# Matmul with batch normalization on one core: the task order as a table, and one block turned by the DMA

## The chip, the core and the metric

The kernel runs on one core of a Trainium2 chip. The metric is device time in microseconds (us), the median of three runs. The profile is of one further execution; its span is the time from its first to its last instruction.

## The reference

```
x: (16, 512, 1024) float32     weight: (1024, 768) float32     gamma, beta: (768,)
y = np.matmul(x, weight)
mean = np.mean(y, axis=(0, 1), keepdims=True)
var = np.var(y, axis=(0, 1), keepdims=True)
y_norm = (y - mean) / np.sqrt(var + eps)
return (gamma * y_norm + beta).astype(np.float32)
```

So it is a product of 8192 by 1024 with 1024 by 768, then every one of the 768 columns is normalized with its mean and variance over all 8192 rows. No value of a column can be written before the last row of that column has been multiplied.

## The kernel before

The 8192 rows of x are 16 chunks (c = 0 to 15) of 512 rows, and the 768 columns are six column tiles (nt = 0 to 5) of 128. x is read with a conversion to bf16 through GpSimd's DMA queue into a buffer called `ring`, transposed there by VectorE into `xT_sb`, and multiplied by the weight in bf16.

Tiles 0 and 1 are multiplied with rows of x as the stationary side while x comes in (line 510); their chunks 14 and 15 are done by columns (line 814) and turned at lines 1064 and 1074. Tiles 2 to 5 have the columns on the partitions (`y_ps` is 128 columns by 512 rows, line 575): each product of a chunk takes eight matmuls, in two tasks of four. VectorE takes the statistics of the chunk (`bn_stats`, line 711; ScalarE for most of tile 2), ScalarE writes it to `y_sb` as bf16 (line 715). When all 16 chunks of a tile are done, the mean and variance give a scale and a shift (`finish_tasks`), and the tile is written out in eight blocks of two chunks, 1024 rows by 128 columns, 512 KB each, while TensorE goes on with the next tile. Tile 5 comes last; nothing of it can leave before its last matmul.

A block has its columns on the partitions and must be turned before it is stored. There are three ways:

- `raw_turn` and `raw_block`: the block is turned before its statistics are known, and normalized afterwards by VectorE (multiply, line 1174) and GpSimd (add, line 1178). `raw_spread` first turns the scale and shift (lines 1141, 1142), gathers and deals them (line 1145) and puts them in PSUM (line 1158).
- `col_block` with mode `pe`: VectorE normalizes in place (line 1026), TensorE turns the block with eight transpositions by the identity (line 1044), ScalarE copies the result from PSUM to a part of `ring` as float32 (line 1210), SP stores it (line 1202). A matmul task can host these transpositions: one is put behind each of its matmuls.
- `col_block` with mode `xact`: VectorE (for tile 2 ScalarE, line 1023) normalizes, SP issues one DMA transposition of the whole block from `y_sb` to a part of `ring` in bf16 (line 1220), ScalarE converts that to float32 in another part of `ring` (line 1232), SP stores it (line 1202).

For tile 4, the fifth column tile, blocks c = 0, 2 and 4 are raw, c = 6, 8, 10 and 12 are of mode `pe`, and c = 14 is held back and stored in two halves at the end of the matmuls (`held_block`, copies at line 1252, stores at line 1255). For tile 3, the blocks c = 2 to 14 are of mode `xact`.

At the end the statistics of tile 5 are joined (line 1308), ScalarE takes the root (line 1311), VectorE the reciprocal and the final pair (lines 1323, 1324), and each block of tile 5 is normalized (line 1348), turned by TensorE (line 1044), copied by ScalarE (line 1361) and stored by SP (line 1364). This is 4 MB that leaves after the last matmul.

`ring` has 6144 words of 4 bytes in each partition. A block's float32 result takes 1024 words, the bf16 result of a DMA transposition 512. A piece is free again when its store has landed.

The order of the work is set while the program is built. Every piece of work is a `Task` with the engines that may do it, its dependencies and a due time. `arrange` goes forward in a planned time: it looks at which engine can begin something first, and among the tasks that could begin on it within 0.2 us takes the one that is due first. The instructions are emitted in that order, so each engine's queue, SP's too, is fixed; an instruction whose data is not there holds up all behind it on its engine.

In the following a task is named by its engine's letter (P for TensorE, V for VectorE, A for ScalarE, G for GpSimd, S for SP) and its number in the order in which the tasks are made. Those used are:

- A562, A566, A570, A574: conversions (line 1232) of blocks c = 8, 10, 12, 14 of tile 3; S563, S567, S571, S575: their stores. S565, S569, S573: DMA transpositions of c = 10, 12, 14.
- V644, A645, A647: the scale and shift of tile 4 turned (lines 1141, 1142), gathered (line 1145), put in PSUM (line 1158). V648, G649, S650: multiply, add and store of raw block c = 0 of tile 4; V651 to S653: c = 2; V654 to S656: c = 4.
- V657, 658, A659, S660: block c = 6 of tile 4, normalized, turned, copied, stored. V661 to S664: block c = 8; V665 to S668: c = 10; V669 to S672: c = 12.
- A684: chunk 6 of tile 5 to `y_sb` (line 715). V691: statistics of chunk 8 of tile 5.
- A725: the root of tile 5 (line 1311). A731 and A734, S732 and S735: copies and stores of the held block.
- S739, S743, S747 and so on: the eleven stores of tile 5.

Of the kernel before, what the change touches and what calls it, by code (L numbers as in the profile page):

```python
# [97 lines left out]
class Wires:  # L98
# [8 lines left out]
    def ready(self, queue):  # L107
        lanes = self.lanes[queue]
        return 0.0 if len(lanes) < self.LANES else lanes[-self.LANES]
# [9 lines left out]
        return t, land  # L119


def arrange(tasks, turns, log=None):

    free = {e: 1.25 for e in ("PE", "DVE", "ACT", "POOL", "SP")}
    wires = Wires()
    port = {"DVE": 0.0, "POOL": 0.0}
    left = sorted(tasks, key=lambda t: t.prio)
    order = []  # L130
    SEM, LOOK = 0.06, 0.2

    def ready(t):
        if t.after is not None and t.after.end is None:
            return None
        r = 0.0
        for d in t.deps:
            if d.end is None:
                return None
            r = max(r, d.end + SEM + t.slack)  # L140
        kept = [(s.pool, s.pool.mark()) for s in t.takes] if len(t.takes) > 1 else []
        fits = True
        for s in t.takes:
            p = s.pool.place(s)
            if p is None:
                fits = False
                break
            r = max(r, p[0] + SEM)
            if kept:
                s.pool.take(s, p[1])  # L150
        for pool, mark in reversed(kept):
            pool.reset(mark)
        if not fits:
            return None
        if t.dma:
            r = max(r, wires.ready(list(t.engines)[0]))
        return r

    def start_of(t, r, e):

        b = max(r, free[e])
        if e == "DVE" and t.lock:
            b = max(b, port["POOL"])
        elif e == "POOL" and not t.dma:
            b = max(b, port["DVE"])
        return b

    while left:
        seen = [(t, ready(t)) for t in left]
        first = {}  # L170
        for t, r in seen:
            if r is not None:
                for e in t.engines:
                    b = start_of(t, r, e)
                    if e not in first or b < first[e]:
                        first[e] = b
        if not first:
            raise RuntimeError(f"nothing can begin: {[(t.prio, t.emit) for t in left[:8]]}")
        e = min(first, key=lambda k: first[k])
        best = None  # L180
        for t, r in seen:
            if r is not None and e in t.engines and start_of(t, r, e) <= first[e] + max(LOOK, t.look):
                if best is None or t.prio < best[1]:
                    best = start_of(t, r, e), t.prio, t
        start, _, t = best
        for s in t.takes:
            s.pool.take(s, s.pool.place(s)[1])
        occ, lat = t.engines[e]
        t.hosted = []
        if t.hosts:  # L190
            room = t.hosts
            for u, r in seen:
                if u in turns and r is not None and r <= start + 0.3 and room >= 1:
                    n = min(room, turns[u][0])
                    if turns[u][0] == turns[u][1]:
                        places = [s.pool.place(s) for s in u.takes]
                        if any(p is None or p[0] > start for p in places):
                            continue
                        for s in u.takes:
                            s.pool.take(s, s.pool.place(s)[1])  # L200
                        u.takes_done, u.takes = u.takes, []
                    t.hosted.append((u, n))
                    turns[u][0] -= n
                    room -= n
                    occ += 0.0555 * n
                    lat += 0.0555 * n
        if t in turns:
            occ = lat = 0.0555 * turns[t][0]
            lat += 0.2
            t.count = turns[t][0]  # L210
        free[e] = start + occ
        if e == "DVE" and t.lock or e == "POOL" and not t.dma:
            port[e] = start + occ
        t.end = start + lat
        if t.dma:
            free[e], t.end = wires.send(e, start, occ, t.dma, t.count)
        t.start, t.engine = start, e
        order.append(t)
        left.remove(t)
        for u, n in t.hosted:  # L220
            if turns[u][0] == 0:
                u.end = t.end + 0.2
                left.remove(u)
    return order


# [1 line left out]
def kernel(  # L228
# [19 lines left out]
    P = 128  # L248
# [24 lines left out]
    XT, YB, SQ = C - EARLY, 28, 3  # L273
    ADDED = (0,6,16,28,40)
    PARTED, LATE, SINGLE = (4,5,7,8,9,10), (12,13,14,15), (2,3,6)
    MODE = {2:'xact',3:'xact',4:('pe',)*8}
    MODE = {nt: m if isinstance(m, tuple) else (m,) * (C // GY) for nt, m in MODE.items()}
    RAW, RAWADD, RAWDUE = {2:(0,2),3:(0,),4:(0,2,4)}, {2:'POOL',3:'POOL',4:'POOL'}, {2:14.0,3:8.0,4:8.0}
    RING = 3 * CH // 32 * KQ // 2
# [85 lines left out]
    def act(occ):  # L365
        return {"ACT": (occ, occ + 0.11)}
# [73 lines left out]
    order = [("x", 0), ("w", 0, 2), ("x", 1), ("w", 2, 4)]  # L440
# [5 lines left out]
    t = 1.0  # L446
# [238 lines left out]
    def y_of(nt, c):  # L685
        return y_col.setdefault((nt, c // GY), Slot(ys))
# [174 lines left out]
    S = clock[0]  # L861
# [94 lines left out]
    k = 0  # L956
# [74 lines left out]
    def turn_block(prio, nt, m0, count, deps, uses):  # L1031

        bank = Slot(banks)
        todo = []

        def step():
            if not todo:
                o_ps = psum.tile([P, count, P], bf16, tag="b")
                bank.tile = o_ps
                for s in range(count):  # L1040
                    c, i = divmod(m0 // P + s, RT)
                    todo.append((o_ps[:, s], y(nt, c)[:, i * P:(i + 1) * P]))
            dst, src = todo.pop(0)
            seq(nc.tensor.transpose(dst, src, ident))  # L1044

        def emit(eng):
            for _ in range(emit.task.count):
                step()

        emit.step = step  # L1050
        t = task(prio, pe(0.0555 * count), emit, deps, takes=[bank], uses=uses)
        emit.task = t
        turns[t] = [count, count]
        return t, bank
# [136 lines left out]
    def col_block(nt, c, due, fin_task, held=False):  # L1191
# [26 lines left out]
        def xbar(eng):  # L1218
# [49 lines left out]
    for nt in range(GA, NT - 1):  # L1268
# [10 lines left out]
        f = finish_tasks(nt)  # L1279
        start = clock[0] + 3.0  # L1280
# [58 lines left out]
    for c, r0, rows in ends:  # L1339
        due = E + 2.0 + 0.6 * c  # L1340
        n = max(rows // CH, 1)
# [13 lines left out]
        b, bank = turn_block(due + 0.6 * (n - 1), nt, m0, count, norms, [y_of(nt, c + i) for i in range(n)])  # L1355
# [7 lines left out]
        def store(eng, slot=slot, m0=m0, count=count):  # L1363
# [48 lines left out]
```

## Time and profile before

| | |
|---|---|
| median of 3 runs | 206.11 us (205.88 to 206.58) |
| span of the profiled execution | 204.1 us |
| around the span, against the median | 2.0 us |
| TensorE busy | 189.3 us (93%) |
| VectorE, ScalarE, GpSimd busy | 159.3, 146.2, 124.1 us |
| DMA: read and written in HBM | 36.71 MB, 25.17 MB |
| last matmul of the product ends | 186.6 us |
| SP issues the first store of tile 5 | 189.31 us |

The times in the profile are microseconds from the first instruction of the profiled execution. The time of that execution outside its span is not given; the difference of 2.0 us between its span and the median of the runs stands for it. The column "DMA" counts the mean busy share of the core's 16 DMA engines, "GB/s" what they moved; in the rows for a window of time they are given in 40 equal slices of that window. A DMA's semaphore is raised in 16 parts, one for each DMA engine, and the DMA has landed with the last of them.

### The profile page before, as it was taken

The numbers are of one execution on the slowest core, as the hardware profiler recorded it, in microseconds if no ns is written. First come the engines' busy times: TensorE is split into PE (matmuls) and PEld (weight loads), VectorE is DVE, ScalarE is ACT, GpSimd is POOL, SyncE is SP. The second block draws the span as 40 slices with busy tenths as digits, with TensorE's granted clock in tenths as the row PEclk, the third lists the DMA queues.
The fourth block names the chain that finished last, engine by engine and source line by source line (L and its number), as shares of the span: only waits on it lengthen the run. The fifth ranks groups of instructions, "written<-read, shape, count | busy, mean of one in ns | idle before, by whom it ended". The sixth has DMA issues, their size and how long they took to land.

```text
span 204.1 us, 3510 instructions
## 1 busy us (share of the span) xinstructions
PE 189.3 (93%) x1210; PEld 114.5 (56%) x1210; DVE 159.3 (78%) x250; ACT 146.2 (72%) x260; POOL 124.1 (61%) x150
## 2 busy tenths in 40 slices
PE   7969999999999999999999999999999999997900
PEld 3457554657488888777865444444444445544600
DVE  4031879999999999969989998987999878657900
ACT  2001461368989999899978766999998959956950
POOL 7776954877499989997403999389613312940000
PEclk9999999999999999999999999999999999999965
DMA  4999999999999999999686899899999999999998
GB/s 71 172 199 196 176 196 196 196 197 197 190 193 197 197 196 196 196 197 195 103 181 200 297 339 336 248 301 328 295 322 227 336 303 274 347 343 310 310 347 253
DMA packets 98562, 48.74 MB, mean 239 GB/s; under 512 B 24304, under 2 KB 98032, under 8 KB 98544
## 3 DMA queue, kind: packets, MB, share of 16 engines
q0 software_dynamic: 34624, 18.36, 65.5%
q1 hardware_dynamic: 63920, 30.16, 52.6%
q8 instruction: 9, 0.15, 0.3%
q14 instruction: 9, 0.07, 0.1%
HBM read 36.71 MB, written 25.17 MB: 303 GB/s over the span
## 4 chain that ended last, share of the span: by engine, by line
PE 86%; ACT 3%; DMA 3%; POOL 2%; issue 1%; ACTq 0%; DVE 0%; POOLq 0%
PE y_ps L575 54%; PE y_ps L510 24%; PE y_ps L814 4%; ACT o_sb L1361 3%; DMA ring<-in_x_dram 3%; PE o_ps L1044 1%; POOL ring L403 1%; POOL w_sb L387 1%; PE y_ps L753 1%; PE a_ps L903 1%; PE o_ps L1074 0%; ACTq L1407 0%; PE idle_ps L591 0%; PE tot_ps L871 0%; ACT ring L1252 0%
## 5 line engine op out<-in xcount | busy, mean ns | idle before, releaser
L575 PEld LDWEIGHTS <-w_sb 128*128 128x128 bf16 x520 | 50.3, 97 | 57.6
L575 PE MATMUL y_ps<-xT_sb,w_sb 128*128 128x512 bf16 (+1 forms) x272 | 59.3, 371 | 0.0
L575 PE MATMUL y_ps<-x_pl,w_sb 128*128 128x512 bf16 x248 | 57.4, 379 | 0.0
L403 POOL DMA_DIRECT2D ring<-in_x_dram x76 | 47.2, 626 | 14.4 <-DMA ring<-in_x_dram 5.5
L510 PE MATMUL y_ps<-w_sb,xT_sb 128*128 128x256 bf16 x448 | 50.6, 273 | 1.7 <-DMA ring<-in_x_dram 1.6
L510 PEld LDWEIGHTS <-xT_sb 128*128 128x128 bf16 x448 | 43.5, 98 | 9.4 <-DVE xT_sb L435 2.9
L435 DVE STREAM_TRANSPOSE xT_sb<-ring 128x1024 f32<-128x1024 f32 (+1 forms) x29 | 31.2, 1111 | 14.1 <-DMA ring<-in_x_dram 13.9
L711 DVE BATCH_NORM_STATS2 stats<-y_ps 128x6 f32<-128x512 f32 x46 | 30.9, 687 | 7.7 <-PE y_ps L575 7.2
L715 ACT CAST y_sb<-y_ps 128x512 bf16<-128x512 f32 x51 | 29.0, 593 | 10.4 <-DVE stats L711 6.3
L547 ACT COPY x_pl<-xT_sb 128x1024 bf16<-128x1024 bf16 x32 | 32.8, 1063 | 1.7 <-DVE xT_sb L435 1.7
L942 POOL TENSOR_TENSOR ring<-ring,sum 128x1024 f32<-128x1024 f32 (+1 forms) x11 | 23.8, 2188 | 14.9 <-ACT y_ps L724 10.9
L659 ACT ACTIVATE sq_sb<-y_ps 128x512 f32<-128x512 f32 x28 | 16.3, 610 | 16.2 <-PE y_ps L510 15.9
L666 POOL TENSOR_TENSOR sum<-sum,sq_sb 128x512 f32<-128x512 f32 x20 | 25.6, 1278 | 3.0 <-ACT sq_sb L659 1.7
L662 DVE TENSOR_TENSOR sum<-y_ps,sum 128x512 f32<-128x512 f32 x28 | 18.9, 675 | 6.3 <-ACT sq_sb L659 5.3
L672 ACT CAST y_sb<-y_ps 128x512 bf16<-128x512 f32 x28 | 16.3, 594 | 8.2 <-DVE sum L662 8.0
L1178 POOL TENSOR_TENSOR ring<-ring,sum 128x1024 f32<-128x1024 f32 x6 | 14.8, 2477 | 9.8 <-issue 8.5
L937 DVE TENSOR_TENSOR ring<-y_sb,a_ps 128x1024 f32<-128x1024 bf16 (+1 forms) x16 | 16.7, 1079 | 0.1
L1044 PE MATMUL o_ps<-ident,y_sb 128*128 128x128 bf16 x104 | 13.1, 221 | 1.6 <-DVE y_sb L1348 1.5
L1232 ACT CAST ring<-ring 128x1024 f32<-128x1024 bf16 x13 | 13.8, 1063 | 0.6 <-DMA ring<-y_sb 0.6
L1145 POOL COPY sum<-sum 32x256 f32<-32x256 f32 (+1 forms) x17 | 5.8, 340 | 13.4 <-DVE sum L1142 6.5
L428 DVE STREAM_TRANSPOSE xT_sb<-ring 128x2048 bf16<-128x2048 bf16 x6 | 13.5, 2290 | 0.1
L591 PE MATMUL idle_ps<-idle_sb 128*128 128x512 f32 x18 | 9.6, 688 | 1.5 <-DVE idle_sb L316 1.5
(104 smaller groups left out, 153.7 us busy)
## 6 DMA issues: line engine op xcount, KB each, us to landing
out_dram<-ring SPq DMA_DIRECT2D x37, 512.0 KB, 3.4
ring<-in_x_dram POOLq DMA_DIRECT2D x52, 256.0 KB, 8.8
out_dram<-o_sb SPq DMA_DIRECT2D x6, 512.0 KB, 4.7
ring<-in_x_dram POOLq DMA_DIRECT2D x16, 128.0 KB, 5.9
w_sb<-in_weight_dram POOLq DMA_DIRECT2D x8, 192.0 KB, 6.2
out_dram<-ring SPq DMA_DIRECT2D x6, 256.0 KB, 3.0
ring<-in_x_dram POOLq DMA_DIRECT2D x4, 192.0 KB, 7.8
out_dram<-o_sb SPq DMA_DIRECT2D x3, 256.0 KB, 2.5
```

The lines of the kernel that those rows point to most:

```text
L403: bi = seq(nc.gpsimd.dma_start(x_bf[32 * i:32 * i + 32], src[:, :, KQ * i:KQ * (i + 1)]))
L435: seq(nc.vector.transpose(dst, src[:, :, jw0:jw1]))
L510: seq(nc.tensor.matmul(y_ps[:, s], x_of(c, jw, e, t * P, (t + 1) * P), w_sb[:, jw, e, 0:NA], start=(s == 0 and jw == 0 and e == 0), stop=( ...
L547: seq(nc.scalar.copy(dst, pairs) if eng == "ACT" else ENG[eng].tensor_copy(dst, pairs))
L575: seq(nc.tensor.matmul(y_ps, w_sb[:, jw, e, nt * P:(nt + 1) * P], moving(c, jw, e, q0 * QR, q1 * QR, parted), start=(jw == 0 and e == 0 an ...
L659: seq(nc.scalar.activation(sq_sb[:, 0:n], slot.tile[:, 0:n], AF.Square))
L662: seq(nc.vector.tensor_add(sum1, slot.tile[:, 0:n], sum1))
L666: seq(ENG[eng].tensor_add(acc, acc, state["sq"][:, 0:n]))
L711: seq(nc.vector.bn_stats(dst, slot.tile))
L715: seq(nc.scalar.copy(y(nt, c), slot.tile))
L937: seq(nc.vector.tensor_mul(slot.o, y_row[c].y[:, s0:s1], aff[0][:, None, :].to_broadcast([P, n, NA])))
L942: seq(ENG[eng].tensor_add(slot.o, slot.o, row[:, None, :].to_broadcast([P, n, NA])))
```

## The change

There are two parts.

The planner's choice is replaced by a table: `ORDER` lists all tasks with their engines, and `arrange` only follows it (it still works out planned times, and the places in the pools). A word such as `P693+666.4` says that the matmul task 693 hosts four transpositions of task 666. Against the order that the planner gave before, the table has these exchanges, and no others apart from the second part:

- TensorE: the matmul P420 ahead of the transpositions P384 of rows of chunk 14 (tiles 0 and 1), at 107 us.
- VectorE: the two normalizations V388, V387 of that block ahead of an addition (line 942) for rows of tiles 0 and 1; one multiplication (line 937) ahead of an addition (line 942); the reciprocal of tile 2's root ahead of one `bn_stats`; a normalization of tile 3 (c = 4) behind a copy to `x_pl` (line 547) and a `bn_stats`, and another such copy behind a normalization and the turned scale and shift of tile 3; V644 ahead of V657; the `bn_stats` of chunk 4 of tile 5 ahead of the normalization of the held block; V691 ahead of V648.
- ScalarE: the root of tile 2 ahead of a line-715 copy; one normalization of tile 2 (line 1023) ahead of a line-715 copy; two line-715 copies ahead of a conversion and a normalization of tile 2; A566 ahead of A684; the root A725 ahead of A731.
- SP: three times a DMA transposition is issued ahead of the store that stood before it (block c = 14 of tile 2, c = 2 and c = 8 of tile 3).
- GpSimd: none.

The second part is the mode of block c = 8 of tile 4, from `pe` to `xact`. Eight transpositions, with their eight loads of weights, leave TensorE's queue, where P689 and P690 (chunk 8 of tile 5) hosted them. SP gets a DMA transposition S662, between S567 and S571. ScalarE's copy A663 from PSUM becomes a conversion from `ring`; the store S664 stays.

```
+ORDER = (
+    "G0 P59 G3 G8 A9 G4 G7 V1 V2 P60 G10 P61 P62 P63 P64 P65 V5 V6 P66 G12 P67 P68 P69 P70 P71 G14 P76 A72 "
...
+    "P697+670.4 V651 S575 A663 P698+670.4 S650 V695 G652 A667 S664 P701 V699 A696 S668 V654 A700 P702 S653 "
...
+)
 def arrange(tasks, turns, log=None):
-    left = sorted(tasks, key=lambda t: t.prio)
+    left = tasks
...
-    while left:
-        seen = [(t, ready(t)) for t in left]
...
-        e = min(first, key=lambda k: first[k])
...
-        start, _, t = best
+    for word in ORDER.split():
+        word, _, riders = word.partition("+")
+        t, e = left[int(word[1:])], NAMES[word[0]]
+        r = ready(t)
+        start = start_of(t, r, e)
...
-        if t.hosts:
-            room = t.hosts
...
+        for rider in riders.split(",") if riders else ():
+            i, n = rider.split(".")
+            u, n = left[int(i)], int(n)
...
-    MODE = {2:'xact',3:'xact',4:('pe',)*8}
+    MODE = {2:'xact',3:'xact',4:('pe','pe','pe','pe','xact','pe','pe','pe')}
```

More of the change, by code (lines that the diff above doesn't have):

```diff
@@ L128, in arrange @@
     port = {"DVE": 0.0, "POOL": 0.0}
-    left = sorted(tasks, key=lambda t: t.prio)
+    left = tasks
     order = []
-    SEM, LOOK = 0.06, 0.2
+    SEM = 0.06
     def ready(t):
@@ L166, in start_of @@
         return b
-    while left:
-        seen = [(t, ready(t)) for t in left]
[L170 to L178, printed above, removed]
-        e = min(first, key=lambda k: first[k])
[L180 to L184, printed above, removed]
-        start, _, t = best
+    NAMES = {"P": "PE", "V": "DVE", "A": "ACT", "G": "POOL", "S": "SP"}
+    for word in ORDER.split():
+        word, _, riders = word.partition("+")
+        t, e = left[int(word[1:])], NAMES[word[0]]
+        r = ready(t)
+        if r is None:
+            raise RuntimeError(f"out of order: {word}")
+        start = start_of(t, r, e)
         for s in t.takes:
@@ L189, in arrange @@
         t.hosted = []
-        if t.hosts:
-            room = t.hosts
[L192 to L206, printed above, removed]
+        for rider in riders.split(",") if riders else ():
+            i, n = rider.split(".")
+            u, n = left[int(i)], int(n)
+            if turns[u][0] == turns[u][1]:
+                for s in u.takes:
+                    s.pool.take(s, s.pool.place(s)[1])
+                u.takes_done, u.takes = u.takes, []
+            t.hosted.append((u, n))
+            turns[u][0] -= n
+            occ += 0.0555 * n
+            lat += 0.0555 * n
         if t in turns:
@@ L218, in arrange @@
         order.append(t)
-        left.remove(t)
         for u, n in t.hosted:
@@ L222, in arrange @@
                 u.end = t.end + 0.2
-                left.remove(u)
     return order
```

36 rows, old and new, of the table ORDER are left out of this document.

## The prediction

> **What bounds the kernel now.** I read the page's slices first, then the chain that ended last, then the DMA rates of the last 47 us in finer slices, then ScalarE's and SP's timelines at 163 to 190 us. From the page:
>
> ```profile
> PE   7969999999999999999999999999999999997900
> DMA  4999999999999999999686899899999999999998
> ```
>
> TensorE is full from the third slice to 186 us, and the DMA engines are full in nearly all of the second half: two resources are candidates. The chain, cut:
>
> ```profile
> 169.34 0.06 PE o_ps L1044
> 169.40 0.22 PE y_ps L575
> ...
> 177.82 6.99 PE y_ps L575 x32
> 184.80 1.81 PE y_ps L753 x16
> ...
> 186.92 0.58 ACT ring L1252
> 187.51 0.20 ACT std L1311
> ...
> 189.60 4.74 ACT o_sb L1361 x6
> ```
>
> The reader sees that a hosted transposition costs TensorE 0.06 us behind each matmul, and that the chain goes through TensorE without a wait up to the tail. Then the DMA from 157 to 177 us, and from 184 to 204 us, in slices of 0.5 us:
>
> ```profile
> GB/s 10 259 348 349 346 286 295 348 349 344 348 347 336 289 308 80 344 349 344 349 348 316 290 284 290 331 348 349 298 290 22 180 347 350 344 349 346 344 347 350
> ```
>
> ```profile
> GB/s 346 344 348 350 344 348 346 258 74 329 284 346 260 247 227 349 344 344 347 348 344 347 350 344 347 348 344 347 350 344 347 348 344 347 350 345 346 132 0 0
> out_dram<-ring SPq DMA_DIRECT2D x1, 512.0 KB, 6.0
> ```
>
> Stores run at 347 GB/s, so 512 KB take 1.51 us; the stretches at 284 to 298 are DMA transpositions. From 172.7 us on the DMA is full, except for dips between 187.5 and 191.5 that sum to 1.1 us of full rate. The last line is S656, issued at 183.56 and landed 6.0 us later, at 189.5, though the rate had dipped at 187.7: in the trace 15 of its 16 parts land by 188.3 and the last at 189.53. One DMA engine lags by 1.3 us. It does so since 180 us, where the DMA rows hold an instruction load (16 KB on one engine in 0.93 us).
>
> So two paths end together. **TensorE path**: the last store that found an empty queue is S747, issued at 190.29; stores start moving 0.92 us after their issue (S567: 171.78, first packet 172.70), then 2 x 0.76 + 6 x 1.51 + 0.76 gives 191.21 + 11.34 = 202.55. **DMA path**: on the lagging engine from 172.70, ten stores of 512 KB (15.1), the lag (1.3) and the last 4.5 MB (13.6, held block and tile 5): 202.7. The last store lands at 203.15, and the span ends 0.95 later at 204.1; the median of the runs is 2.0 above the span. All below are differences, so 206.11 is the base.
>
> **TensorE's part.** The program has eight matmul-transpositions and eight weight loads fewer on TensorE. From the chain a matmul with its rider takes 0.06 + 0.22 (0.273 from start to start over 169.34 to 177.82), one alone 6.99 / 32 = 0.218: 8 x 0.055 = 0.44 us less, all of it on the path, since nothing of TensorE waits there. P420 ahead of P384 takes a wait for VectorE off: starts there are 0.21 us late in all, I take 0.05, bounds 0 and 0.2. The other exchanges make banks come free up to 0.6 us later (a line-715 copy takes 0.58) or earlier; TensorE has no late start between 108 and 186.8 us, so the cover is its spare banks. I take 0; without the cover 0.6. TensorE path: -0.5.
>
> The root A725 now goes ahead of A731. Joined statistics end at 187.37 and the root begins at 187.41, so it gains nothing and keeps 0.2 us of ScalarE from A731: S732, issued at 187.53, comes at about 187.72 with everything 0.5 earlier. From its first packet at 188.64 the 13.6 us run without a break: 202.25. TensorE path with this: -0.45.
>
> **The DMA's part.** S662 adds a transposition. Queued ones land 0.85 to 1.1 us after what stood before them, and stores behind them 1.3 to 1.45 instead of 1.51: net 0.9, on the path because the queue is never empty after it. VectorE: DVE Perf Modes, in the Trainium skill, section "The three transpose paths", prices a 128 by 128 transposition at 1309 ns by the DMA and 390 ns by TensorE; eight would be 10.5 us and the sum 215. The trace contradicts it: eight pass in 0.9 us here, and in 0.44 on TensorE; I keep no chance for it.
>
> What the table gives back: the gap of 0.62 us at 172.08 to 172.70, where S567 waited for A566.
>
> ```profile
> 168.16 0.58 ACT L715 CAST y_sb<-y_ps 128x512 bf16<-128x512 f32 x1 [0.21 <-DVE stats L711]
> 169.07 1.00 ACT L1145 COPY sum<-sum 32x64 f32<-32x64 f32 x4 [0.32 <-DVE sum L1142]
> 170.11 0.58 ACT L715 CAST y_sb<-y_ps 128x512 bf16<-128x512 f32 x1
> 170.72 1.04 ACT L1232 CAST ring<-ring 128x1024 f32<-128x1024 bf16 x1
> ```
>
> ScalarE waited 0.32 us for V644, which now goes ahead of a normalization of 0.5; A566 (170.72) also passes A684, whose place took 0.61. So A566 starts about 169.75 (its transposition landed at 169.23), S567 goes out at 170.8 and its data at 171.7, before the queue is empty. The gap closes: -0.62. Bounds: 0 and -0.62.
>
> Upstream, three transpositions pass a store that waits for a conversion (SP waited 0.6 to 1.5 us for each), and 0.4 us of rate are missing around 144. Since the queue is full from there to 172 but for a stall at 156 and a dip at 164.5, half a microsecond at most can be handed down. I take -0.3, bounds 0 and -0.45. The remaining exchanges of the first half touch a DMA that is idle half of 100 to 112 us: nothing, at worst 0.6 on stores with 20 us in hand.
>
> Behind S662 on SP's queue stand S571, S660, S575, S650. SP holds a transposition 1.3 to 2.4 us; from 171.2 it is done by 173.0 to 173.6, when A570 ends (173.03), and the queue has work to 174.5. Nothing, at worst 0.1. A663 becomes a conversion: 1.06 against 1.01, the same place. V661 ends at 170.5, so S662 does not wait.
>
> DMA path: 0.9 - 0.62 - 0.3 = 0.0, so 206.1. The TensorE path would give -0.45, 205.65. The later one decides: **no change**, 206.1, own range 205.7 to 206.6.
>
> **Rival 1, faster: the DMA keeps slack and TensorE's time comes through.** For it: the dips of 1.1 us at 187.5 to 191.5 are more than 0.9. Against: they are the mean of 16 engines, and the lagging one has none. It needs the lag to shrink or the upstream gain to be at its bound. Then 205.65, or with the full 0.2 at P384 and the 0.15 by which the DMA path is the longer one now, 205.3. I set 205.4 with a chance of 0.30, four fifths of it beyond the bound. Runtime: NRT & Kernel Launch, in the Trainium skill, section "Instruction fetch mechanics", has crossing a 16 KiB block of instructions "mostly hidden"; by that the 1.3 us of lag would not count, and this rival would win at 205.65. The landing in parts above contradicts it for a full queue.
>
> **Rival 2, slower: the first raw store comes late.** V691 now stands ahead of V648. V648 began at 172.34, V691 can only begin when chunk 8 is multiplied (173.47, less 0.45), so V648 begins near 173.6, GpSimd's addition (2.36 us) ends near 177.3, and S650, issued at 176.31 before, goes at 177.4. The queue has work from 172.08 for 0.9 + 4 x 1.51, to 179.0, so S650 must be out by 178.1: 0.7 us in hand. S662 takes 1536 of the 6144 words of `ring` some 2 us earlier than A663 took its 1024; VectorE waited at line 1174 up to 0.7 us for a store to land already. One more landing, 1.51 us, puts S650 at 178.9, and the queue stands empty 0.8; with V651 and GpSimd's two further additions behind it I put 1.0: 207.1. Chance 0.20.
>
> **Rival 3: the gap at 172.08 stays**, if A566 is not earlier (its transposition lands later, or ScalarE waits elsewhere): the DMA path is +0.6, 206.7. Chance 0.05, half of it beyond the bound. That the change does not do what it says is out: the built program has 20 transpositions on SP and 2343 rows on TensorE instead of 2359.
>
> **How the numbers follow.** The forecast has 0.45, all within 0.3% (0.6 us, about what a measurement of this kernel tells from no change). Faster: 0.24 from rival 1. Slower: 0.20 from rival 2 and 0.03 from rival 3. Within: 0.45 + 0.06 + 0.02 = 0.53. The range goes from rival 1's best, 205.3, to rival 2, 207.1.
>
> **What would show it.** Right: TensorE's last matmul of line 753 ends 0.45 to 0.6 earlier; no slice below 300 GB/s between 171 and 187 but for one transposition at about 290; S567 issued near 170.8; the first slices of the tail without a dip on the lagging part, and the last store landing at 203.15 within 0.4. Wrong: a dip of half a microsecond or more at 178 to 181 (rival 2); an end at 202.7 with landings in step (rival 1); a matmul that starts late before 186 us, or an instruction load that falls into S662, as one fell into a transposition at 155.6 and stopped the DMA for 1.4 us.

## The result, and the profile after

| kernel | median, us | lowest and highest | executions |
|---|---|---|---|
| before | 206.16 | 205.88 to 206.58 | 6 |
| after | 207.17 | 206.47 to 207.56 | 6 |

The ratio is 1.0056, 95% interval 1.0038 to 1.0074: the changed kernel is slower by 1.0 us, where no change was forecast. The profiled execution of after has a span of 205.8 us and took 207.56, the longest of its six. In after, line numbers are 24 higher than before (575 is now 599, 814 is 838, 1202 is 1226, 1407 is 1431).

Before the traces can be compared they need a common zero. The first matmul of the product began at 12.14 us before and at 12.57 after, and the last matmul of line 814 (838 after), up to which TensorE's queue is the same in both, at 104.66 and 105.31. Over three profiled executions of the changed kernel that second mark lies at 105.31, 104.30 and 104.42, so these 0.65 us differ from execution to execution and say nothing of the change. **All marks below are counted from that matmul.** "Spacing" is the time from one DMA's landing to the next one's in the same queue, taken where 14 of the 16 parts have landed, so that one late DMA engine does not hide the others; "the last landing" is that of all 16 parts of the last store.

The busy rows of the page, after:

```profile
PE   7969999999999999999999999999999999996700
DMA  5999999999999999999685998989999999999995
```

TensorE is as full as before, and its last slices fall earlier. The chain that ended last, after, cut to its end:

```profile
168.25 1.67 PE y_ps L599 x7
...
171.88 1.94 PE y_ps L599 x9
...
184.94 1.83 PE y_ps L777 x16
186.80 0.45 DVE fin L784
187.26 0.26 DVE mv L1332
187.55 0.30 ACT std L1335
...
189.75 4.74 ACT o_sb L1385 x6
```

The last matmul of line 777 (753 before) is at 81.17 where it was at 81.68: 0.51 us earlier. That part came as forecast. The chain does not show the stores behind it; the DMA rows do, shifted by the 0.65 us so that they stand beside those of before (157.65 to 177.65 and 184.65 to 204.65, slices of 0.5 us):

```profile
GB/s 9 66 307 346 348 325 290 315 347 347 317 291 322 348 352 342 347 348 344 348 348 313 233 283 231 312 347 348 318 291 318 347 346 287 272 313 348 347 344 349
```

```profile
GB/s 347 348 344 349 348 344 347 348 248 245 344 343 345 339 345 345 345 348 349 344 347 346 346 348 349 344 347 346 347 347 349 344 347 346 348 346 222 37 19 0
```

The gap of 22 and 180 GB/s in the middle of the first row of before is gone. But that row begins with 9 and 66 where before's had 10 and 259: a stop of the DMA ends about a third of a microsecond later. In the second row the dips near 191 are gone, and the row does not break off but ends in 37 and 19 GB/s. ScalarE, whose wait made the gap:

```profile
168.75 0.59 ACT L739 CAST y_sb<-y_ps 128x512 bf16<-128x512 f32 x1 [0.78 <-DVE stats L735]
169.24 1.00 ACT L1169 COPY sum<-sum 32x64 f32<-32x64 f32 x4
170.26 1.05 ACT L1256 CAST ring<-ring 128x1024 f32<-128x1024 bf16 x1
171.22 0.58 ACT L739 CAST y_sb<-y_ps 128x512 bf16<-128x512 f32 x1
```

The wait of 0.32 for V644 has gone, and A566 (line 1256) passes A684 (the second copy of line 739). A566 begins at 170.26, which is 64.95 on the common scale; the forecast, 169.75, was 65.09 there.

The end, for 202 to 206 us in slices of 0.1, before and then after:

```profile
GB/s 338 348 343 358 343 348 256 57 0 0 0 0 0 0 0 0 0 0 0 0 0 0 0 0 0 0 0 0 0 0 0 0 0 0 0 0 0 0 0 0
```

```profile
GB/s 348 338 338 353 348 343 348 348 333 159 67 67 67 31 20 20 26 20 20 20 21 0 0 0 0 0 0 0 0 0 0 0 0 0 0 0 0 0 0 0
```

Full rate is 348, so one of 16 engines alone moves 21.7: the 67 GB/s are three DMA engines that still work, the 20 a single one that works on when the others are done. Before, all end together. Of the last store, 14 of the 16 parts have landed at 98.31 (98.43 before), 15 at 98.39 (98.47), and the last at 99.12 (98.49): +0.63.

And there is a third piece. The instructions of SP at line 1407 (1431) are the program's end: count, shortest, median and longest duration in ns, first and last start. Before and after:

```profile
L1407 SPq EVENT_SEMAPHORE  x11: 17/28/28, 199.9 to 204.0; - x11
L1407 SPq DRAIN  x3: 7/7/7, 203.2 to 203.5; - x3
```

```profile
L1431 SPq EVENT_SEMAPHORE  x11: 17/28/28, 200.7 to 205.7; - x11
L1431 SPq DRAIN  x3: 7/7/7, 204.9 to 205.3; - x3
```

The first drain stands at 203.2, just behind the last landing (203.15), before; after, at 204.9, half a microsecond behind it (204.44). From the last landing to the end of the span it is 0.92 before and 1.35 after: +0.43. So, from the common mark on, the profiled execution lost 0.63 at the landing and 0.43 behind it, 1.06 in all, beside 1.01 in the medians.

**The end in detail.** SP's DMAs use eight semaphores in turn, and at the end SP waits for the eight in a fixed order, some 0.06 us for each. Before, SP issues 88 DMAs and the last store is on the semaphore waited for last. The added transposition makes 89, the last store moves on to the one waited for first, and the other seven waits, long satisfied, are passed one by one after it has landed, from 204.45 to 204.88 in the trace.

**The stop of the DMA.** The trace has a 16 KB load of TensorE instructions on one DMA engine at 155.58 us before, and at 156.79 after. The rates for 150 to 162 us, slices of 0.3, before and after:

```profile
GB/s 288 292 309 349 348 350 345 313 292 290 306 346 348 348 350 304 290 290 326 265 87 14 6 9 10 244 303 348 348 350 346 319 292 288 300 350 348 346 348 343
```

```profile
GB/s 348 352 350 336 352 350 343 348 332 293 290 279 281 208 285 323 340 350 335 338 278 267 102 0 0 4 9 9 154 283 348 352 346 346 343 287 289 288 339 352
```

Before, the load is met by a transposition, whose spacing is 2.34 instead of 0.95. After, it is met by the store ahead of a transposition (S549 now stands ahead of S485, so other DMAs are in flight when the load comes); that store's spacing is 3.48 instead of 1.5, a loss of 2.0 us where it was 1.4. These two stops, and the ones that the experiments below find, are read as the work of the load because they move with it when the load alone is moved (E10 to E12, E17).

### The profile page after: what moved, and what is told of

It is laid out like the page before. It is cut to its first block, busy times and chain, and to the rows that moved or that the text cites. A ratio compares the mean times of both kernels' runs of the same rounds, so it can differ in the third digit from the quotient of the medians.

```text
span 205.8 us, 3480 instructions
## 1 busy us (share of the span) xinstructions
PE 188.3 (92%) x1188; PEld 114.3 (56%) x1202; DVE 159.5 (78%) x250; ACT 146.1 (71%) x260; POOL 124.3 (60%) x150
## 4 chain that ended last, share of the span: by engine, by line
PE 78%; DMA 9%; ACT 3%; POOL 2%; DVE 1%; issue 1%; ACTq 0%; DVEq 0%; POOLq 0%
PE y_ps L599 50%; PE y_ps L534 21%; DMA w_sb<-in_weight_dram 6%; PE y_ps L838 4%; ACT o_sb L1385 3%; DMA ring<-in_x_dram 3%; PE o_ps L1068 1%; POOL ring L427 1%; PE y_ps L777 1%; POOL w_sb L411 1%; DVE xT_sb L459 1%; PE a_ps L927 1%; ACTq L1431 0%; PE o_ps L1098 0%; PE tot_ps L895 0%
## 5 line engine op out<-in xcount | busy, mean ns | idle before, releaser
L599 PE MATMUL y_ps<-xT_sb,w_sb 128*128 128x512 bf16 (+1 forms) x264 | 58.4, 371 | 0.4
L599 PE MATMUL y_ps<-x_pl,w_sb 128*128 128x512 bf16 x242 | 56.5, 379 | 0.3
L1256 ACT CAST ring<-ring 128x1024 f32<-128x1024 bf16 x14 | 14.7, 1050 | 1.1 <-DMA ring<-y_sb 1.0
L1068 PE MATMUL o_ps<-ident,y_sb 128*128 128x128 bf16 x96 | 11.3, 221 | 1.6 <-DVE y_sb L1372 1.5
```

The source lines that it names most:

```text
L599: seq(nc.tensor.matmul(y_ps, w_sb[:, jw, e, nt * P:(nt + 1) * P], moving(c, jw, e, q0 * QR, q1 * QR, parted), start=(jw == 0 and e == 0 an ...
```

## The experiments

Two theories were set against each other. Theory D: the DMA queue sets the end, by one lagging DMA engine, and the semaphores at the end come on top. Theory T: TensorE and ScalarE set it, through the held store S732 and the first stores of tile 5. Then the upstream loss was tested for its cause.

Every run was timed beside the kernel before on the same chip; ratios are to that, with 95% intervals. E1 to E4, E5 to E8, E9 to E12, E13 to E16, and E17 with E18 each shared a chip. Marks are those of one profiled execution of each kernel, medians and ratios of all its executions. "Load" is the largest spacing near the 16 KB load, S for a store, T for a transposition; "573" is the landing of S573, tile 3's last transposition, ahead of which lies all that is upstream; "S732" is its issue.

| run | DMAs | load | 573 | S732 | last landing | landing to end | median, us | ratio |
|---|---|---|---|---|---|---|---|---|
| before | 88 | T 2.34 | 67.85 | 82.87 | 98.49 | 0.92 | 206.16 | 1 |
| after | 89 | S 3.48 | 68.15 | 83.03 | 99.12 | 1.35 | 207.17 | 1.0056 [1.0038, 1.0074] |
| E1 | 88 | S 3.75 | 68.46 | 83.03 | 99.22 | 0.93 | 206.10 | 1.0014 [0.9998, 1.0030] |
| E2 | 89 | T 2.37 | 68.41 | 82.87 | 98.55 | 1.35 | 206.34 | 1.0030 [1.0013, 1.0047] |
| E3 | 88 | S 3.86 | 68.55 | 83.48 | 98.65 | 0.92 | 205.93 | 0.9999 [0.9981, 1.0017] |
| E4 | 89 | T 2.31 | 68.07 | 82.42 | 99.99 | 1.35 | 207.98 | 1.0105 [1.0079, 1.0132] |
| E5 | 89 | S 3.67 | 68.37 | 83.03 | 99.28 | 1.35 | 206.64 | 1.0041 [1.0025, 1.0057] |
| E6 | 89 | S 3.38 | 68.09 | 82.36 | 98.84 | 1.35 | 207.01 | 1.0059 [1.0041, 1.0076] |
| E7 | 89 | S 3.63 | 68.24 | 83.03 | 98.32 | 1.35 | 205.97 | 1.0015 [1.0000, 1.0030] |
| E8 | 88 | S 3.42 | 68.11 | 82.81 | 98.41 | 0.93 | 205.68 | 0.9996 [0.9983, 1.0010] |
| E9 | 89 | T 2.35 | 67.70 | 83.02 | 98.85 | 1.35 | 206.77 | 1.0038 [1.0026, 1.0050] |
| E10 | 89 | T 2.48 | 67.49 | 83.03 | 98.42 | 1.36 | 206.62 | 1.0043 [1.0023, 1.0063] |
| E11 | 88 | S 2.65 | 68.03 | 82.87 | 98.60 | 0.92 | 206.24 | 1.0019 [1.0006, 1.0032] |
| E12 | 88 | T 2.50 | 67.71 | 82.81 | 98.41 | 0.92 | 205.83 | 0.9995 [0.9986, 1.0005] |
| E13 | 89 | S 3.54 | 68.11 | 83.02 | 99.05 | 1.35 | 206.94 | 1.0047 [1.0030, 1.0064] |
| E14 | 88 | T 2.36 | 68.30 | 83.03 | 99.08 | 0.93 | 206.18 | 1.0003 [0.9991, 1.0015] |
| E15 | 88 | T 2.36 | 67.63 | 82.36 | 98.55 | 0.92 | 205.97 | 0.9999 [0.9985, 1.0012] |
| E16 | 88 | T 2.34 | 67.40 | 82.36 | 98.50 | 0.92 | 206.27 | 1.0005 [0.9993, 1.0017] |
| E17 | 89 | T 2.48 | 67.60 | 83.03 | 98.41 | 1.36 | 206.54 | 1.0032 [1.0011, 1.0053] |
| E18 | 88 | T 2.40 | 67.85 | 82.36 | 98.98 | 0.92 | 206.09 | 1.0007 [0.9987, 1.0028] |

**E1, the changed kernel with one DMA fewer.** `PAIRED` says how many pairs of gamma's six column tiles are loaded with one DMA instead of two.

```
-    PAIRED = 1
+    PAIRED = 2
```

> The changed kernel with one small DMA fewer at the start: gamma's columns 2 and 3 are loaded by one DMA instead of two, so SP issues 88 DMAs as before the change, not 89. Theory of the semaphores: at the end SP waits for its eight DMA semaphores in a fixed order, one wait in 0.06 us; with 89 DMAs the last store has the semaphore that is waited for first, and seven further waits stand behind its landing. With 88 it is the last one again: the stretch from the last landing to the end of the span goes from 1.36 back to 0.95 us, and the median from 207.17 to about 206.75. Rival, all of the loss is in the DMA engines or in the order: no change from 207.17 but for noise of 0.2.

**E2, the kernel before with one DMA more.**

```
-    PAIRED = 1
+    PAIRED = 0
```

> The kernel before, with one small DMA more at the start: gamma's columns 0 and 1 are loaded by two DMAs, so SP issues 89, and nothing else differs. Theory of the semaphores: the last store's semaphore is waited for first, the stretch from the last landing to the end of the span goes from 0.95 to 1.36 us, and the median is 0.4 above the kernel before, at 206.55. Rival: within 0.15 of the kernel before.

The rows of the program's end, E2 and then E1:

```profile
L1407 SPq EVENT_SEMAPHORE  x11: 17/28/28, 200.1 to 204.4; - x11
L1407 SPq DRAIN  x3: 7/7/7, 203.6 to 203.9; - x3
```

```profile
L1431 SPq DRAIN  x3: 7/7/12, 204.9 to 205.3; - x3
```

E2's last store lands at 203.10 and its first drain is at 203.6; E1's lands at 204.85, with the drain right behind it. The cost moved with the number of DMAs in both directions. In the times, E2 is 0.48 us above the kernel before on its chip (0.4 was expected); E1, at 1.0014, lies further below the changed kernel (1.0041 to 1.0056 in three sets of runs) than the 0.42 us expected. E1's profile is of the longest of its twelve executions (207.56), so its late landing stands beside a median of 206.10. In the table the time from landing to end is 0.92 or 0.93 us in all ten kernels with 88 DMAs, and 1.35 or 1.36 in all ten with 89.

**E3, the exchanges alone:** the block turned by TensorE. **E4, the turn alone:** the order of before, with S662 between S567 and S571.

```
 E3:  -  ... A647 S567 S662 P690 ...   P689
      +  ... A647 S567 P690+662.4 ...  P689+662.4     and the mode 'pe' again
 E4:  +  ... S567 S662 A570 ... put into the order of before, and the mode 'xact'
```

> The table with its exchanges, but block c = 8 of tile 4 turned by TensorE as before. Theory of the DMA path: without the transposition (0.9 us on the DMA engines) and with the gap at 172 us closed, the DMA path is 0.6 shorter than that of the kernel before, and TensorE's path, 0.1 to 0.2 shorter there, decides: 205.9 to 206.1. If instead the exchanges are what costs, 206.8 or more. TensorE's last matmul: 0.45 later than in the changed kernel, from the same mark at 105 us.

> The order of the kernel before, with the transposition of block c = 8 of tile 4 by the DMA put between S567 and S571 and the eight transpositions taken from TensorE. Theory of the DMA path and of the semaphores together: +0.9 from the transposition on a queue that is full from 172 us to the end, +0.4 from the last semaphore: 207.4, with the gap at 172 us still there. If the exchanges carry the loss: 206.2 or less.

E4 lands 1.5 us later than before and E3 0.16 later. E3's time is in the range of its theory; E4's, 207.98, is 0.6 above what was expected. The end of E4 (198 to 206 us, slices of 0.2):

```profile
GB/s 343 353 343 353 333 353 343 353 343 353 343 346 346 346 351 343 353 343 353 333 353 343 336 100 56 38 20 23 20 23 20 10 0 0 0 0 0 0 0 0
```

Of the 1.5 us only 0.16 is on 14 of the 16 parts (98.59 against 98.43); 1.40 is the lag of the last one behind them, the long stretch of 20 GB/s. The kernel before has such a lag too, 1.2 on S656, but it shrinks to 0.06 by the end: the other engines wait for TensorE in the dips of the tail, and there the late one can catch up. E4's lag was larger to begin with, 1.6 to 1.8, behind a 16 KB load that took 1.47 us where it took 0.93 before, so not all of its 1.5 us is the change's. With the transposition the queue is full when S732 comes, and the lag stays. So the transposition's own 0.9 us show on the late engine; the others only lose waits. E3, without the transposition, has no lag left (98.62 and 98.65). There S732 is issued 0.6 late because root A725 goes ahead of A731; whether that sets the end is what E8 asks.

**E5, the changed kernel again; E6, with A731 ahead of A725; E7, with S656 cut in half; E8, E3 with A731 ahead of A725.**

```
 E6, E8:  - A725 A731 S732
          + A731 A725 S732
 E7 (the second half of block c = 4 of tile 4 is not written):
          +            k = n // 2 if (nt, c) == (4, 4) else n
          -                out_flat[m0:m0 + n * P, ...], slot.o))
          +                out_flat[m0:m0 + k * P, ...], slot.o[:, 0:k]))
```

> The changed kernel as it is, to stand beside the next three on one chip. Both theories expect the ratio to the kernel before found already, 1.004 to 1.007, so 206.9 to 207.3 us, the last landing about 99.1 us behind the last line-838 matmul and the span's end 1.36 after it.

> The changed kernel with the held block's first copy A731 ahead of the root A725 again, as before. That lets the held store S732 go 0.5 to 0.6 us earlier. Theory D (the DMA queue is full to the end on its lagging engine): the last landing stays 99.1 behind the last line-838 matmul, within 0.15, and the time stays at that of the changed kernel, within 0.2 us. Rival T (TensorE's and ScalarE's path through S732 sets the end): landing and time 0.5 us lower.

> The changed kernel with the store S656 cut to its first half (256 KB instead of 512, still one DMA, so the turn of the semaphores is the same; half of that block is not written). Theory D: 0.75 us less to move ahead of the held store, so the lag of one DMA engine is mostly absorbed before it; last landing at 98.4 instead of 99.1, time 0.65 to 0.75 us below the changed kernel, 206.3 to 206.5. Rival T: S732 is issued as before and the end is the same within 0.15 us.

> The exchanges of the table with the block turned by TensorE (88 DMAs), and A731 ahead of A725. In the run with the exchanges alone all 16 DMA engines ended together (98.62 and 98.65) and S732 was issued at 83.48, 0.6 later than in the kernel before: there the path through S732 set the end, so the exchange of root and copy cost what the others gave. Theory: S732 at 82.9, last landing at 98.1 to 98.2, time 205.3 to 205.6, faster than the kernel before by 0.4 to 0.6 us. Rival (the exchanges close the gap and nothing comes through because the lag of 1.3 us stays to the end): landing at 98.5 to 98.7, time as before, 205.9.

E6: S732 is 0.67 earlier, 14 parts of the last store have landed at 97.98 instead of 98.17 in E5, and the landing is 0.44 lower than in E5, more than theory D allowed, but the time is not lower (207.01 and 206.64, intervals overlap). Of the 0.44, 0.28 is there already at 573 (68.09 and 68.37), far ahead of the exchange; from there to the last landing E6 takes 30.75 us and E5 30.91. E7: 256 KB less ahead of S732, and the rates at 184 to 204 us (slices of 0.5) show the dips of the tail again and no stretch of 20 GB/s:

```profile
GB/s 346 346 345 350 349 344 315 69 79 336 283 345 343 260 345 344 345 346 345 346 349 349 345 346 345 347 348 349 346 345 345 349 346 349 347 344 210 0 0 0
```

The lag dissolves in them, the landing is at 98.32 and the time 0.67 lower than E5's, in the range of theory D; theory T had no change. In this chip's runs that is the plainest: the changed kernel is bound by the DMA queue. E8 put S732 where it was expected, 0.67 earlier than in E3, but the landing only came down by 0.24, to 98.41, and the time is that of before: a miss. So S732 alone did not set E3's end. In E8 TensorE still has the eight transpositions: its last matmul is at 81.62, where E15 below has 81.17, and tile 5's first store is issued at 84.59 instead of 84.14, with dips of the DMA rate around it. The 0.4 us between E8 and E15 or E16 in the landing of 14 parts (98.37, then 97.94 and 97.96) is what turning the block by the DMA takes off TensorE.

The traces of all twenty kernels settle it between the two theories. From the landing of the last part of S656 to the last landing it is 13.60 to 13.63 us in sixteen of them, before and after among them, with S732 issued anywhere from 82.36 to 83.03: the late engine works through its share of the last 4.5 MB without a break (13.6 us at 1.51 for 512 KB), as theory D has it. It is 13.66 in E7, and 13.94 to 13.98 in E3, E8 and E12; only in these three does the path of theory T add something. So with the transposition and the gap closed all that is late upstream comes through: in twelve kernels (E7 apart) the last landing follows 573 by 30.75 to 31.15 us. In the order of before the wait for A566 lies between: before, E2 and E11 have 573 at 67.85 to 68.41 and land at 98.49 to 98.60.

**E9, S485 ahead of S549 again. E10 and E12, the load moved by 24 instructions of TensorE; E11, the same for before, by 12.** E12 is E8 with that edit.

```
 E9:        - ... S640 ... S549 ... S485 S553
            + ... S640 ... S485 S549 ... S553
 E10, E12:  -    SMALL = 8     (small warming matmuls)
            +    SMALL = 20
 E11:       +    SMALL = 14
```

> The changed kernel with one store ahead of one transposition again: S485 before S549 on SP's queue, as before the change. In seven runs with the table's order the 16 KB instruction load at 51.5 us behind the last line-838 matmul falls on the store between two transpositions, and that store lands 3.4 to 3.9 us after the transposition ahead of it instead of 1.45; in three runs with the order of before the load falls on a transposition, which takes 2.3 to 2.4 instead of 0.95. Theory (that place of the load is the upstream loss of 0.5 to 0.9 us): the spacing of 3.4 to 3.9 goes, a transposition of 2.3 to 2.4 stands in its place, and the last landing is 98.4 to 98.7 instead of 99.1 to 99.3; time 0.4 to 0.8 us below the changed kernel. Rival (the loss comes from transpositions following each other, wherever the load falls): landing 99.1 to 99.3, time unchanged within 0.2.

> The changed kernel, its table untouched, with 20 small warming matmuls at the start instead of 8: 24 more TensorE instructions ahead of all others, in time in which TensorE waits for data. At about 0.1 us an instruction each of TensorE's 16 KB loads comes 2.2 to 2.6 us earlier in the work: the one at 51.5 behind the last line-838 matmul at about 49, where two transpositions are on the DMA. Theory: the spacing of 3.4 to 3.9 us falls to 2.3 to 2.5 in that neighbourhood, the last landing to 98.3 to 98.6, the time 0.5 to 0.8 us below the changed kernel. Rival: nothing changes, 99.1 to 99.3.

> The kernel before with 14 small warming matmuls instead of 8, so that its 16 KB load at 50.9 behind the last line-814 matmul comes about 1.1 us earlier and falls on the store at 49.2 to 50.7, which is followed by a transposition, as in the changed kernel. Theory: that store or the transposition behind it takes 2.0 us or more too long instead of 1.4, the gap of 0.6 at 172 (a wait for ScalarE) takes the difference up, and the last landing moves by 0.1 or less: 98.4 to 98.6; time as before within 0.3. Rival (the place of the load costs to the end in this kernel too): landing 99.0, time up by 0.5.

> The exchanges of the table with the block turned by TensorE, A731 ahead of A725, and 20 small warming matmuls. Without the last edit it landed its last store at 98.41, and lost 2.0 us at the instruction load. Theory: the load's place gives 0.5 to 0.8 us, of which the path through S732 (issued at 82.8, from its first packet 13.6 us) lets 0.3 through: landing at 97.9 to 98.2, time 205.1 to 205.5, faster than the kernel before by 0.5 us. Rival (nothing comes through): 98.4, 205.7.

All four moved the stop as expected: in E9, E10 and E12 a transposition of 2.35 to 2.50 stands in place of the store of 3.4 to 3.9, and in E11 a store of 2.65 in place of the transposition of 2.34 (1.2 too long, less than the 2.0 expected; its landing and time stayed in the range of the theory). The table's order without a repair (after, E1, E3, E5, E6, E7, E8, E13) has 573 landed at 68.09 to 68.55, mean 68.26; the table's order with the load moved (E9, E10, E12, E14 to E18) at 67.40 to 68.30, mean 67.71. So the place of the load costs 0.55 us at that point. The landing followed in part: 98.85 and 98.42 in E9 and E10, against 99.05 to 99.28 of the changed kernel's three executions, and E12, which was to land at 97.9 to 98.2, did not go below 98.41: a miss. The times of E9 and E10, which were to be 0.4 to 0.8 us lower, did not follow beyond their intervals: misses too. In E10's profile the product's first matmul, at 12.59 us, waits for no DMA, the twelve further warming matmuls had ended just then. That this is the reason is not shown: in E12, with the same edit, it begins at 11.54, and E10's mark, 104.62, is no later than that of before.

**E13, the changed kernel a third time; E14, both costs taken away (`PAIRED = 2` and `SMALL = 20`); E15, E14 with A731 ahead of A725; E16, E9 with `PAIRED = 2` and A731 ahead of A725.**

> The changed kernel as it is, to stand beside the next three on one chip: 1.004 to 1.006 of the kernel before, a spacing of 3.4 to 3.9 us at the 16 KB load, 1.30 to 1.39 us from the last landing to the end of the span.

> The changed kernel with both disputed costs taken away and nothing else: 20 small warming matmuls, so that the 16 KB load falls on a transposition, and gamma loaded with one DMA fewer, so that the last store is on the semaphore that is waited for last. Theory (the two together are the whole difference): landing 98.3 to 98.6, 0.92 to 0.97 from there to the end, time that of the kernel before within 0.2 us and 0.6 to 1.0 below the changed kernel. Rival (the load's place does not reach the time, as the runs that moved the load alone showed ratios like the changed kernel's): only the 0.4 of the semaphores, ratio 1.002 to 1.004.

> As the run before, and A731 ahead of A725, so that the held store S732 goes 0.6 us earlier, at 82.4. Theory: 15 DMA engines end at 97.9 instead of 98.26 as in the run with A731 ahead alone, and with the lag at 0.2 to 0.9 the landing is 98.1 to 98.6; time 205.5 to 206.0, 0 to 0.4 us faster than the kernel before. Rival (the lagging engine sets the end whatever S732 does): 0.2 us or less between this run and the one before it.

> The changed kernel with S485 ahead of S549, A731 ahead of A725, and gamma with one DMA fewer: the load's place moved by the table instead of by the warming matmuls. Theory: as the run before, landing 98.1 to 98.7, time 205.5 to 206.1. Rival (the warming matmuls had another effect): 0.4 us or more above the run before.

E14 is 0.76 us below E13, and within 0.0015 of the kernel before: the two costs together are nearly the whole difference in time. Its one profile was the slowest of its twelve executions and landed later than expected (99.08); it has a further dip of 0.6 us near 162.7, and E18 one like it near 159.9, whose cause stays open. E15 and E16 agree with each other (0.3 us, overlapping intervals) and with the kernel before: 14 parts of the last store have landed at 97.94 and 97.96, half a microsecond ahead of before, but the late one holds the landing at 98.5. What the exchange of root and copy would give is given to the lag.

**E17, the load moved with a shorter warming; E18, with all edits.**

```
-    WAKE = 8
+    WAKE = 7
-    SMALL = 8
+    SMALL = 21
 E18 also: PAIRED = 2, and A731 ahead of A725
```

> The changed kernel with seven large and 21 small warming matmuls at the start instead of eight and 8: the 16 KB load comes as early as in the run with 20 small ones, but the warming ends about 1.2 us sooner than there, where in the profile the first matmul of the product began only when the warming had ended (12.59) and not when its data had come. Theory: a transposition of 2.3 to 2.5 us at the load, first matmul released by a DMA again, and the time 0.2 to 0.5 us below the changed kernel (1.002 to 1.0035 of the kernel before), the rest being the 0.42 of the semaphores. Rival (the load's place does not reach the time): 1.004 to 1.0055, as the changed kernel.

> The same warming, gamma with one DMA fewer, and A731 ahead of A725: all that was found, on the changed kernel. Theory: landing 98.4 to 98.6 behind the last line-838 matmul (15 DMA engines at 97.9), 0.95 from there to the end, time 0 to 0.4 us below the kernel before, 0.998 to 1.000. Rival: as with 20 small ones, 0.9999.

The rates of E17 at 150 to 162 us, slices of 0.3:

```profile
GB/s 345 342 352 345 346 348 341 291 288 287 303 187 9 3 9 10 151 285 347 352 352 341 345 285 288 288 342 350 346 343 353 284 291 289 336 346 343 350 353 287
```

The stop is now met by a transposition and is 1.4 us wide instead of 2.0, as before the change. The ratio, 1.0032, is in the expected range, but its interval reaches to those of the changed kernel. E18 is not faster than the kernel before (1.0007, where 0.998 to 1.000 was expected), nor was any other version clear of its interval.

**What stays open** is how the 1.0 us splits in time. Against the changed kernel's 1.0041 to 1.0056, taking the load away gave 1.0032 to 1.0043 (0.1 to 0.3 us below the mean of the three), taking the semaphore away 1.0014 (0.7 us, where the traces show 0.43). The sum is settled, by E14 and by the traces: behind the common mark the span ends at 100.40 to 100.63 in the three executions of the changed kernel, and at 99.40 and 99.52 in before and E11. The two shares are settled only to 0.3 us in the times, since the executions of one kernel lie 0.5 to 1.9 us apart.

## Why the prediction was wrong, point by point

- **TensorE, -0.5: right.** The last matmul of line 777 is 0.51 earlier, and S732 was put at 187.72, 83.06 on the common scale: 83.03.
- **The transposition, +0.9: right.** S567, the store behind the gap, divides the sum well. From its landing to the last landing it is 28.38 to 28.52 us in three executions with the order of before (before, E2, E11), and 29.37 to 29.41 in the three of the changed kernel (after, E5, E13): +0.95. It is on the late engine, as the prediction had it; in after, 14 of 16 parts show 0.2 of it.
- **"Upstream ... I take -0.3, bounds 0 and -0.45", and with it the gap's -0.62: this step failed.** The two were to bring S567's landing 0.92 earlier. S567 was to be issued at 66.14, and was at 66.12; after's trace has no gap there. But the queue ahead of it was late. S567 landed at 70.05 to 70.17 in four executions with the order of before (before, E2, E4, E11), and at 69.53 to 70.09, mean 69.80, in eight with the table's order (after, E1, E3, E5 to E8, E13): 0.29 earlier, a third of the forecast. What the exchanges give was sized rightly: with the load moved it lands at 69.03 to 69.13 in six (E9, E10, E12, E15, E16, E17), 1.0 earlier, and at 69.40 and 69.85 in E18 and E14 with their further dip. A load falls into that stretch, and the step took its stop of 1.4 us as fixed. It depends on what is in flight, and the exchanges change just that. By 573 alone the place of the load costs 0.55; the +0.30 there between the profiles of before and after is one execution each, and the order of before spreads from 67.85 to 68.41, which its wait for A566 hides. The prediction named the risk, for S662 only.
- **"the span ends 0.95 later": the second failure, a term that was left out.** The time from landing to end was carried over as a constant; it is 0.43 longer with 89 DMAs. In sum: +0.95 for the transposition, -0.3 where -0.92 was forecast, and +0.43 that was not forecast make 1.1 us; the medians have 1.0.
- **The path through TensorE and S732 was sized about right, and did not decide.** Its 202.25 is the end of the data; the landing comes 0.45 later (202.7 and 203.15 in the prediction), so at 98.04 on the common scale. Where this path does decide, in E8 and E12, TensorE's last matmul (81.62) and S732 (82.81) stand nearly as in before, and the landing is at 98.41; the prediction's 202.55 for before is 98.34 by the same reckoning. In all kernels with the turn by the DMA the late engine ends later than 98.04, at best at 98.32 (E7), so rival 1 (205.4) had next to no room.
- **Rival 2 had the number but not the way.** Its 207.1 is close to 207.17, yet S650 was issued at 73.59 (it "must be out by" 73.44 on this scale), and the spacing there is 1.57 instead of 1.51: it cost less than 0.1.
- **The DMA path by the lagging engine: right.** The prediction let the last 4.5 MB take 13.6 us there, without a break; the traces have 13.62 before and 13.63 after. The lag behind the other engines, taken as 1.3 us, was misread by a little: at S656 14 parts, not 15, had landed by 188.3, the 15th at 188.86 and the last at 189.53, a lag of 1.2. In after it was 1.4 to 1.5, and 0.8 from the tail to the end; before, it was gone by the end. (A slip without weight: with eight blocks at 1309 ns the sum is 215.7 by its own terms, not 215.)
- The Trainium skill, Runtime: NRT & Kernel Launch, section "Instruction fetch mechanics", has the crossing "mostly hidden". The chain of after shows no wait of TensorE over 0.06 us near the load at 156.8, but the full DMA queue stops: for 1.4 us with a transposition in flight, and 2.0 us with a store ahead of one.

## What to carry to other kernels

Where the DMA queue is full, an order is not only a matter of sums: look in the trace for the instruction loads, and at what stands in the queue when they come, since a reordering that saves 0.3 us can put one where it costs half a microsecond more. Count the DMAs of the queue that ends the program: one more or less can move the last store to another place in the waits at the end. And when a trace shows one late DMA engine, follow that engine: dips in the mean rate of all 16 are no slack if the late one works through them.

## What was not expected of the hardware

- The eight waits at the program's end: 0.92 or 0.93 us from the last landing to the end of the span with 88 DMAs on SP, 1.35 or 1.36 with 89, in ten kernels each.
- A 16 KB instruction load that takes 0.9 to 1.2 us on one DMA engine stopped the others for 1.4 to 1.6 us when a transposition was in flight, and added 1.9 to 2.4 to a store that a transposition followed in eight kernels, 1.2 in a ninth (E11).
- A lag of 0.8 us on one DMA engine kept its size over 12 us of a full queue.
